# Sparse attention's projections in another order: index block first, one query block of 512 columns, score scratch in another pool

## The chip, the cores and the metric

The kernel runs on one core of a Trainium2 chip. A core has five engines, each with its own instruction queue that it works through strictly in the order in which the program was built: TensorE (PE in the profile; its weight loads are PEld), VectorE (DVE), ScalarE (ACT), GpSimd (POOL) and SyncE (SP, which here only starts transfers). Engines wait for one another by semaphores. The metric is the device time of one execution in microseconds (us).

## The reference

Two layers of a decoder trunk over 512 tokens of width 1024, in float32. Cut to what matters here:

```python
h = rmsnorm(x, norm_mix)
(a_x, a_b, a_c, d_q, d_k, d_v, i_q, i_k, i_w, ..., m_q, gate_logits) = split_cols(h @ w_in)
y_a = a_b * causal_conv3(a_c * a_x, conv_w)             # branch A
# branch B, sparse attention, for each block of 128 queries:
rel   = relu(iq . ik * 64**-0.5)                        # 8 index heads
score = sum over heads of rel * iw                      # (128, keys), causal
sel   = top_k(score, 128)                               # the 128 best keys of each query
out   = softmax(q . k[sel] / 8) @ v[sel]                # 8 heads of 64
# branch C: gated recurrence; branch M: cross-attention into 256 memory tokens
merged = sum over the branches of sigmoid(gate) * (y_branch @ w_lift)
x = x + merged @ w_out
x = x + (silu(gate) * up) @ ffn_w_down                  # feed-forward
```

Columns of `w_in` that belong to sparse attention: 512 for the queries `d_q`; 64 + 64 for `d_k` and `d_v`; 512 + 64 + 8 for the indexer `i_q`, `i_k`, `i_w`.

## The kernel before

Every product of the two operands' full precision is three matmuls of rounded halves (`mm3`, L324, L325, L327: high by high, low by high, high by low). A weight chunk (`Chunk`, made by `wchunk`) is loaded by SP into `w_raw`, ACT rounds it to `w_hi` (L100, the line of the helper `A`), and DVE makes the remainder `w_lo` (L257). There are 4 buffers of `w_raw` and 3 each of `w_hi` and `w_lo`. `features` computes with weights as the stationary operand, 512 tokens moving; `tokens` and `tokens_wide` with a tile of 128 tokens as the stationary operand and the weight's columns moving, so that a matmul is as wide as the chunk has columns.

In a layer's `mixer` several generators are woven together. `script(EARLY[l], ...)` names one step per letter: `b` projections of sparse attention, `c` convolution branch, `m` memory branch, `s` a step of the selection, `n` (layer 1 only) the late norm. After it, `lift(3, ...)` (gates and lift of the memory branch; four rounds of 48 gate matmuls on h and 24 on y) is woven with what is left of the selection, and then `values` and `lift(0, ...)` with `attend(0)` to `attend(3)`.

- `projections` has a key block of 256 columns (`d_k`, `d_v` and the first two index heads), an index block of 456 columns, and the queries as two blocks of 256. Each block's results are scaled out of PSUM by ACT into a tile `wide` (4 buffers) and then normalised, rotated and turned per head (`key_heads`, `index_heads`, `query_heads`; mostly DVE, with transposes on PE).
- `select(t)`, for t = 1 to 3, works on n = 128(t+1) keys. For each of 8 heads: a product of two matmuls on PE (`dots`, L841 and L842, into a PSUM tile `at`, 2 buffers), a relu by ACT into a scratch tile, and one DVE instruction that adds it to `score` (L994, L996). Then 16 rounds on DVE of MAX8 (L1002) and MATCH_REPLACE8 (L1003), and a mask `bias` (L1006).
- `attend(t)` makes logits (`dots` again, on `qS` and `k`), then on DVE the maximum with mask (L857), on ACT the exponential, on DVE a reciprocal (L860), on ACT the scaling of `prob`, and on PE its transposes (L871). The first of them stands on PE behind the first half of the first gates of `lift(0)`.

All of this gives only the priorities. The order in which instructions stand on each engine is set when the program is built, by a scheduler with a timeline of its own (`TileContext(nc, schedule_with_timeline_sim=True)`); instructions under `tc.high_priority` come earlier, and `tc.add_manual_dep(..., order)` pins single pairs. On the chip nothing is reordered.

Of the kernel before, what the change touches and what calls it, by code (L numbers as in the profile page):

```python
# [16 lines left out]
AF = mybir.ActivationFunctionType  # L17
# [6 lines left out]
NT = S // P  # L24
D = 1024
KD = D // P
# [11 lines left out]
C_AX, C_AB, C_AC, C_DQ, C_DK, C_IQ, C_IK = 0, 512, 1024, 1536, 2048, 2176, 2688  # L38
# [3 lines left out]
NONC = -2.0e38  # L42
OFF = -1.0e30
AHEAD = 3000
EARLY = ["mmbmcmcbmmmscsmcsssmccmbs", "mnmbmcmcbmmmscsmcsssmccmbs"]
MM_BUFS = 3
TR_BUFS = 3
AT_BUFS = 2
# [23 lines left out]
def hybrid_trunk(ctx: ExitStack, tc: tile.TileContext, x, mem, positions, norm_mix, w_in, conv_w,  # L72
# [33 lines left out]
    def mm_ps():  # L106
        return pmm.tile([P, 512], F32, name="mm")
# [4 lines left out]
    def tr_ps():  # L112
        return pat.tile([P, 512], F32, name="tr", bufs=TR_BUFS)
# [32 lines left out]
    ps = tr_ps()  # L146
# [16 lines left out]
    ps = tr_ps()  # L163
# [64 lines left out]
    class Chunk:  # L228
        def __init__(self, src, kt, n):
            self.kt, self.step = kt, min(kt, 1024 // n)  # L230
            self.parts = []
            for k in range(0, kt, self.step):
                e = min(kt, k + self.step)
                m = (e - k) * n
                raw, hi, lo = (wpool.tile([P, 1024], dt, name=nm, bufs=b)[:, :m].rearrange("p (k n) -> p k n", n=n)
                               for nm, dt, b in (("w_raw", F32, RAW_BUFS), ("w_hi", F32R, W_BUFS), ("w_lo", F32R, W_BUFS)))
                if len(src.shape) == 2:
                    loaded[0] = nc.sync.dma_start(raw, src[k * P:e * P].rearrange("(k p) n -> p k n", p=P))
                    raw_loads.append(loaded[0])
                    if len(raw_loads) == 2:  # L240
                        tc.add_manual_dep(mem_half.ins, loaded[0].ins.name, order, reason="weights first")
                    if keys:
                        tc.add_manual_dep(loaded[0].ins, keys.pop().ins.name, order, reason="keys first")
                else:
                    for g in range(2):
                        nc.sync.dma_start(raw.rearrange("p k (g c) -> p k g c", g=2)[:, :, g, :], src[:, k:e, g, :])
                with tc.high_priority(offset=AHEAD):
                    if len(raw_loads) == 1:
                        dve.tensor_copy(hi[:, 1:, :], raw[:, 1:, :])
                        i = A(hi[:, :1, :], raw[:, :1, :], AF.Copy)  # L250
                    else:
                        i = A(hi, raw, AF.Copy)
                    while len(self.parts) == 1 and before_second:
                        tc.add_manual_dep(i.ins, before_second.pop().ins.name, order, reason="probabilities first")
                    while behind:
                        tc.add_manual_dep(i.ins, behind.pop().ins.name, order, reason="accumulators first")
                    i2 = dve.tensor_sub(lo, raw, f(hi))  # L257
                    while low_after:
                        tc.add_manual_dep(low_after.pop().ins, i2.ins.name, order, reason="weights first")
                    while low_behind:  # L260
                        tc.add_manual_dep(i2.ins, low_behind.pop().ins.name, order, reason="operands first")
                    while after_hi:
                        tc.add_manual_dep(after_hi.pop().ins, i.ins.name, order, reason="weights first")
                    for a in after_two:
                        tc.add_manual_dep(a.ins, i.ins.name, order, reason="weights first")
                    for a in after_los:
                        tc.add_manual_dep(a.ins, i2.ins.name, order, reason="weights first")
                self.parts.append((range(k, e), hi, lo))
            after_two.clear()
            after_los.clear()  # L270
# [9 lines left out]
    def wchunk(src, kt, n):  # L280
        return Chunk(src, kt, n)
# [17 lines left out]
    def tokens(w, a, t, ps, k0=0, kt=None, first=0):  # L299
        kt = w.kt if kt is None else kt  # L300
        for k in range(k0 + first, k0 + w.kt):
            mm3(ps, pair(a, k, slice(t * P, (t + 1) * P)), w.at(k - k0), k == 0, k == kt - 1)
# [52 lines left out]
    def scratch512(n):  # L355
        return state.tile([P, S], F32, name="sq", bufs=2)[:, :n]
# [93 lines left out]
    h = new_h()  # L450
# [183 lines left out]
    def mixer(l, h, norms, cm):  # L634
# [197 lines left out]
        with pool_("dsa") as dp:  # L832
# [60 lines left out]
            with pool_("idx") as ip:  # L893
# [5 lines left out]
                def wide():  # L899
                    return ip.tile([P, S], F32, name="wide", bufs=4)  # L900
# [63 lines left out]
                def index_out(ps, t):  # L964
                    u = wide()
                    with tc.high_priority(offset=AHEAD):
                        A(u[:, :7 * HD], ps[:, :7 * HD], AF.Copy, scale=r_t[:, t:t + 1])
                        A(iw[:, t, :], ps[:, 7 * HD:7 * HD + 8], AF.Copy, scale=r8_t[:, t:t + 1])
                    return u

                def index_heads(u, t):
                    w = by_head(u)
                    rope(w[:, :7], 7, t)
                    dve.tensor_copy(w[:, 7, :], w[:, 6, :])
                    ps = turn_heads(u, 4)
                    twin_to(ikS, ps[:, 3 * P:], t)
                    heads_to(iqS, 2, ps[:, :3 * P], 6, t)

                def query_heads(u, t):
                    w = by_head(u)  # L980
                    headnorm(w, 8, gq_b[l])
                    rope(w, 8, t)
                    heads_to(qS, 0, turn_heads(u, 4), 8, t)

                def select(t):
                    n = (t + 1) * P
                    score = ip.tile([P, S], F32, name="score", bufs=1)[:, :n]
                    for hh in range(8):
                        ps = at_ps()[:, :n]
                        dots(ps, iqS, ikS, hh, t, n)  # L990
                        rel = wide()[:, :n]
                        A(rel, ps, AF.Relu, scale=HD ** -0.5)
                        if hh == 0:
                            dve.tensor_scalar(score, rel, iw[:, t, 0:1], 0.0, op0=OP.mult, op1=OP.add)  # L994
                        else:
                            dve.scalar_tensor_tensor(score, rel, iw[:, t, hh:hh + 1], score, op0=OP.mult,  # L996
                                                     op1=OP.add)
                    dve.copy_predicated(score[:, t * P:], future, neg.to_broadcast([P, P]))
                    yield
                    for i in range(TOPK // 8):  # L1000
                        m8 = ip.tile([P, 16], F32, name="m8", bufs=2)[:, :8]
                        dve.max(m8, score)  # L1002
                        dve.match_replace(score, m8, score, REPL)  # L1003
                        if i % 4 == 3:
                            yield
                    dve.tensor_scalar(biases[t], score, REPL, OFF, op0=OP.not_equal, op1=OP.mult)  # L1006

                def projections():
                    w = wchunk(w_in[l][:, C_DK:C_DK + 256], KD, 256)
                    for t in range(NT):  # L1010
                        ps = mm_ps()[:, :256]
                        tokens(w, h, t, ps)
                        key_heads(key_out(ps, t), t)
                    yield
                    w = wchunk(w_in[l][:, C_DK + 256:C_DK + 712], KD, 456)
                    pss = [mm_ps()[:, :456] for _ in range(MM_BUFS)] + [tr_ps()[:, :456]]
                    tokens_wide([w], h, KD, pss, in_turn=True)
                    for t, u in enumerate([index_out(ps, t) for t, ps in enumerate(pss)]):
                        index_heads(u, t)
                    yield  # L1020
                    us = [wide() for _ in range(NT)]
                    for c in range(2):
                        w = wchunk(w_in[l][:, C_DQ + c * 256:C_DQ + (c + 1) * 256], KD, 256)
                        for t in range(NT):
                            ps = mm_ps()[:, :256]
                            tokens(w, h, t, ps)
                            with tc.high_priority(offset=AHEAD):
                                A(us[t][:, c * 256:(c + 1) * 256], ps, AF.Copy, scale=r_t[:, t:t + 1])
                            if c:
                                query_heads(us[t], t)  # L1030
                    yield

                y_m, y_a = new_y(), new_y()
# [651 lines left out]
```

## Time and profile before

| | |
|---|---|
| median of 3 runs | 1975.92 us (1974.9 to 1976.09) |
| profiled execution | 1974.79 us, span 1972.8 us |
| granted PE clock | 0.998 of full speed |
| PE busy | 99% of the span, 9687 matmuls |
| DVE busy | 74% |
| ACT busy | 59% |
| POOL busy | 12% |
| transfers | 385.25 MB, mean 195 GB/s |

Matmuls are pipelined and the profile models their ends, so one matmul's duration (0.39 us for 512 columns) is longer than the distance from its start to the next one's start; what a matmul costs in a full queue is that distance. Instructions of DVE and ACT overlap a little at their ends as well, and are read the same way. Layer 0's mixer lies between about 70 and 690 us, layer 1's between about 1024 and 1640 us.

### The profile page before, as it was taken

What the parts mean: (1) busy time and instruction counts of PE and PEld (TensorE: products, weight loads), DVE (VectorE), ACT (ScalarE), POOL (GpSimd) and SP (SyncE); (2) the same over time, 40 slices, a digit from 0 to 9 for tenths busy, and PEclk for the clock granted to TensorE, in tenths of its full rate; (3) what the DMA queues carried; (4) which work ended last, traced back from release to release, by engine and by line L of the source; (5) the groups of instructions that cost most, each with busy time, mean ns of one, the idle gap of its engine ahead of it and who ended that gap; (6) DMA issues with size and microseconds to landing.
All of it is one profiled execution on the core that took longest, in us unless ns stands there. A gap on an engine that the chain in (4) does not pass through costs nothing.

```text
span 1972.8 us, 26656 instructions
## 1 busy us (share of the span) xinstructions
PE 1958.9 (99%) x9687; PEld 1636.0 (83%) x9687; DVE 1466.6 (74%) x2569; ACT 1169.3 (59%) x1958; POOL 236.2 (12%) x288
## 2 busy tenths in 40 slices
PE   9999999999999999999999999999999999999999
PEld 8888987878888888888888898878888888888887
DVE  7866998657876677786876699965678667867777
ACT  6754654766765456645654556477667655656564
POOL 1011111111111111100001111111111110111000
PEclk9999999999999999999999999999999999999999
DMA  8677666667687888886677767677777778898754
GB/s 304 207 179 168 172 160 166 161 139 172 166 210 186 231 232 255 244 245 188 202 218 168 181 144 174 148 182 157 167 177 162 209 198 251 250 266 235 213 186 139
DMA packets 222228, 385.25 MB, mean 195 GB/s; under 512 B 13194, under 2 KB 118224, under 8 KB 221840
## 3 DMA queue, kind: packets, MB, share of 16 engines
q1 hardware_dynamic: 163008, 244.16, 39.3%
q0 software_dynamic: 52192, 132.81, 33.3%
q10 hardware_dynamic: 6896, 6.58, 1.0%
q8 instruction: 76, 1.25, 0.3%
q14 instruction: 56, 0.46, 0.1%
HBM read 368.81 MB, written 140.51 MB: 258 GB/s over the span
## 4 chain that ended last, share of the span: by engine, by line
PE 97%; DVE 3%; ACT 0%; issue 0%; DVEq 0%; ACTq 0%
PE mm L327 24%; PE mm L324 23%; PE mm L325 23%; PE at L324 4%; PE at L325 4%; PE at L327 4%; PE tr L324 2%; PE tr L327 2%; PE tr L325 2%; PE tr L871 1%; PE tr L882 1%; PE tr L1577 1%; DVE score L1003 1%; PE at L842 1%; PE at L841 1%; DVE m L1002 1%
## 5 line engine op out<-in xcount | busy, mean ns | idle before, releaser
L100 ACT ACTIVATE w_hi<-w_raw 128x1024 fp32r<-128x1024 f32 (+1 forms) x435 | 457.3, 1054 | 353.1 <-PE mm L325 113.3
L324 PE MATMUL mm<-h_hi,w_hi 128*128 128x512 f32 x960 | 377.4, 394 | 0.6 <-DVE zg L1076 0.6
L325 PE MATMUL mm<-h_lo,w_hi 128*128 128x512 f32 x960 | 376.6, 392 | 0.0
L327 PE MATMUL mm<-h_hi,w_lo 128*128 128x512 f32 x960 | 374.8, 397 | 0.7 <-DVE w_lo L257 0.7
L1288 DVE TENSOR_TENSOR w_lo<-w_raw,w_hi 128x1024 fp32r<-128x1024 f32 x211 | 256.3, 1218 | 130.0 <-ACT w_hi L100 129.3
L257 DVE TENSOR_TENSOR w_lo<-w_raw,w_hi 128x1024 fp32r<-128x1024 f32 (+1 forms) x224 | 272.2, 1217 | 105.4 <-ACT w_hi L100 103.9
L1303 POOL DMA_DIRECT2D up_sums<-in_ffn_w_up_dram x120 | 121.5, 1012 | 836.5 <-DMA up_sums<-in_ffn_w_up_dram 554.6
L327 PEld LDWEIGHTS mm<-h_hi,w_lo 128*128 128x128 f32 x960 | 182.7, 190 | 37.6 <-DVE w_lo L257 0.8
L324 PEld LDWEIGHTS mm<-h_hi,w_hi 128*128 128x128 f32 x960 | 180.4, 188 | 36.3 <-issue 1.0
L325 PEld LDWEIGHTS mm<-h_lo,w_hi 128*128 128x128 f32 x960 | 180.4, 188 | 35.6 <-issue 0.2
L325 PE MATMUL mm<-w_lo,h_hi 128*128 128x512 f32 (+2 forms) x488 | 169.4, 347 | 0.3 <-DVE w_lo L257 0.3
L327 PE MATMUL mm<-w_hi,h_lo 128*128 128x512 f32 (+2 forms) x488 | 169.5, 347 | 0.0
L324 PE MATMUL mm<-w_hi,h_hi 128*128 128x512 f32 (+2 forms) x488 | 163.8, 347 | 0.0
L1303 POOL DMA_DIRECT2D w_sums<-in_ffn_w_down_dram x66 | 62.3, 944 | 331.8 <-DMA w_sums<-in_ffn_w_down_dram 186.2
L325 PEld LDWEIGHTS mm<-w_lo,h_hi 128*128 128x128 f32 x488 | 92.3, 189 | 11.3 <-DVE w_lo L257 0.6
L324 PEld LDWEIGHTS mm<-w_hi,h_hi 128*128 128x128 f32 x488 | 92.3, 189 | 10.5 <-ACT w_hi L100 0.2
L327 PEld LDWEIGHTS mm<-w_hi,h_lo 128*128 128x128 f32 x488 | 92.3, 189 | 10.2
L100 ACT ACTIVATE prob<-prob,small 128x128 f32<-128x128 f32 (+3 forms) x128 | 68.8, 554 | 33.6 <-DVE small L857 24.5
L327 PE MATMUL mm<-y_hi,w_lo 128*128 128x512 f32 x192 | 75.5, 393 | 0.0
L325 PE MATMUL mm<-y_lo,w_hi 128*128 128x512 f32 x192 | 75.4, 393 | 0.0
L324 PE MATMUL mm<-y_hi,w_hi 128*128 128x512 f32 x192 | 75.4, 393 | 0.0
L325 PE MATMUL mm<-w_lo,a_hi 128*128 128x512 f32 x160 | 63.2, 395 | 0.0
(496 smaller groups left out, 4191.6 us busy)
## 6 DMA issues: line engine op xcount, KB each, us to landing
w_raw<-in_w_in_dram SPq DMA_DIRECT2D x140, 512.0 KB, 4.6
up_sums<-in_ffn_w_up_dram POOLq DMA_DIRECT2D x120, 512.0 KB, 7.0
w_raw<-up_sums SPq DMA_DIRECT2D x80, 512.0 KB, 5.3
w_raw<-in_ffn_w_up_dram SPq DMA_DIRECT2D x60, 512.0 KB, 4.6
w_sums<-in_ffn_w_down_dram POOLq DMA_DIRECT2D x54, 512.0 KB, 6.1
up_sums<-up_sums POOLq DMA_DIRECT2D x40, 512.0 KB, 5.1
w_raw<-in_w_lift_dram SPq DMA_DIRECT2D x32, 512.0 KB, 4.6
w_raw<-in_ffn_w_down_dram SPq DMA_DIRECT2D x24, 512.0 KB, 5.0
```

What stands on the lines that cost most here:

```text
L100: i = act.activation(dst, src, func, **kw)
L257: i2 = dve.tensor_sub(lo, raw, f(hi))
L324: made += [pe.matmul(ps, ah, bh, start=first, stop=False, skip_group_check=more), pe.matmul(ps, ah, bl, start=False, stop=False, skip_grou ...
L325: pe.matmul(ps, ah, bl, start=False, stop=False, skip_group_check=more)]
L327: made += [pe.matmul(ps, al, bh, start=False, stop=last, skip_group_check=more)]
L841: return [pe.matmul(ps, q[:, hh, s], k[0][:, :n], start=True, stop=False), pe.matmul(ps, q[:, hh, s], k[1][:, :n], start=False, stop=True)]
L842: pe.matmul(ps, q[:, hh, s], k[1][:, :n], start=False, stop=True)]
L871: turn = pe.transpose(pp[:, (2 * e + i) * P:(2 * e + i + 1) * P], probs[2 * i + e][:, b * P:(b + 1) * P], ident)
L882: i = pe.matmul(pv[e * HD:(e + 1) * HD, c], vt[:, b, :], pt[:, b, e * 2 * P:(e + 1) * 2 * P], start=b == 0, stop=b == t)
L1002: dve.max(m8, score)
L1288: two = A(hi, raw, AF.Copy), dve.tensor_sub(lo, raw, f(hi))
L1303: i = nc.gpsimd.dma_start(dst, src, **kw)
```

## The change

The index block comes first, then the key block. The queries become one block of 512 columns over four accumulators (three `mm` tiles and one `tr` tile of PSUM), taken out by a new function `query_out`, and each token tile's `query_heads` is a step of its own, so that steps of other branches can lie between. The scratch of the relu in `select` moves from the pool `wide` (4 buffers) to `scratch512`, a tile `sq` with 2 buffers. The two letter strings change, and the pinned orders `after_two` and `after_los` hold only for a chunk's first part.

```diff
-EARLY = ["mmbmcmcbmmmscsmcsssmccmbs", "mnmbmcmcbmmmscsmcsssmccmbs"]
+EARLY = ["mbmmbcmmmsccbsmcmsssmmsbbcbbc", "mnbmmbcmmmsccbsmcmsssmmsbbcbbc"]
...
-                    for a in after_two:
+                    for a in after_two if len(self.parts) < 2 else []:
                         tc.add_manual_dep(a.ins, i.ins.name, order, reason="weights first")
-                    for a in after_los:
+                    for a in after_los if len(self.parts) < 2 else []:
                         tc.add_manual_dep(a.ins, i2.ins.name, order, reason="weights first")
...
+                def query_out(ps, t):
+                    u = wide()
+                    with tc.high_priority(offset=AHEAD):
+                        A(u, ps, AF.Copy, scale=r_t[:, t:t + 1])
+                    return u
...
-                        rel = wide()[:, :n]
+                        rel = scratch512(n)
                         A(rel, ps, AF.Relu, scale=HD ** -0.5)
...
                 def projections():
+                    w = wchunk(w_in[l][:, C_DK + 256:C_DK + 712], KD, 456)
+                    pss = [mm_ps()[:, :456] for _ in range(MM_BUFS)] + [tr_ps()[:, :456]]
+                    tokens_wide([w], h, KD, pss, in_turn=True)
+                    for t, u in enumerate([index_out(ps, t) for t, ps in enumerate(pss)]):
+                        index_heads(u, t)
+                    yield
                     w = wchunk(w_in[l][:, C_DK:C_DK + 256], KD, 256)
...
-                    w = wchunk(w_in[l][:, C_DK + 256:C_DK + 712], KD, 456)
-                    pss = [mm_ps()[:, :456] for _ in range(MM_BUFS)] + [tr_ps()[:, :456]]
+                    w = wchunk(w_in[l][:, C_DQ:C_DQ + 512], KD, 512)
+                    pss = [mm_ps() for _ in range(MM_BUFS)] + [tr_ps()]
                     tokens_wide([w], h, KD, pss, in_turn=True)
-                    for t, u in enumerate([index_out(ps, t) for t, ps in enumerate(pss)]):
-                        index_heads(u, t)
-                    yield
-                    us = [wide() for _ in range(NT)]
-                    for c in range(2):
-                        w = wchunk(w_in[l][:, C_DQ + c * 256:C_DQ + (c + 1) * 256], KD, 256)
-                        for t in range(NT):
-                            ps = mm_ps()[:, :256]
-                            tokens(w, h, t, ps)
-                            with tc.high_priority(offset=AHEAD):
-                                A(us[t][:, c * 256:(c + 1) * 256], ps, AF.Copy, scale=r_t[:, t:t + 1])
-                            if c:
-                                query_heads(us[t], t)
+                    for t, u in enumerate([query_out(ps, t) for t, ps in enumerate(pss)]):
+                        yield
+                        query_heads(u, t)
                     yield
```

How the built order changes is shown at two places of layer 0; layer 1 reads the same way. The first is PE at the last two products of `select(3)`, its seventh and eighth head. Before, they stand within the lift (`y` operands) of the last round of `lift(3)`, ahead of all matmuls of `values`:

```order
L325 MATMUL mm_3394<-y_lo_796,w_hi_3389 128x512
L327 MATMUL mm_3394<-y_hi_795,w_lo_3390 128x512
L324 MATMUL mm_3394<-y_hi_795,w_hi_3389 128x512
L841 MATMUL at_3024<-ik_hi_791,iqS_790 128x512
L842 MATMUL at_3024<-ik_lo_792,iqS_790 128x512
L841 MATMUL at_3030<-ik_hi_791,iqS_790 128x512
L842 MATMUL at_3030<-ik_lo_792,iqS_790 128x512
L325 MATMUL mm_3394<-y_lo_796,w_hi_3389 128x512
L327 MATMUL mm_3394<-y_hi_795,w_lo_3390 128x512
L324 MATMUL mm_3395<-y_hi_795,w_hi_3389 128x512
```

Now they stand on PE behind three quarters of `values` (`w`, `h` operands; `w_hi_3347` belongs to the fourth and last part of its weights):

```order
L841 MATMUL at_2920<-ik_hi_791,iqS_790 128x512
L842 MATMUL at_2920<-ik_lo_792,iqS_790 128x512
L324 MATMUL tr_3355<-w_hi_3341,h_hi_146 128x512
L325 MATMUL tr_3355<-w_lo_3342,h_hi_146 128x512
L327 MATMUL tr_3355<-w_hi_3341,h_lo_147 128x512
L324 MATMUL mm_3352<-w_hi_3347,h_hi_146 128x512
L324 MATMUL mm_3353<-w_hi_3347,h_hi_146 128x512
L841 MATMUL at_2926<-ik_hi_791,iqS_790 128x512
L842 MATMUL at_2926<-ik_lo_792,iqS_790 128x512
L324 MATMUL mm_3354<-w_hi_3347,h_hi_146 128x512
```

Counted in 512-column matmuls, 142 stood between the eighth product and the first `prob` transpose of `attend(0)` (14 of the lift, 96 of `values`, 32 of the first gates); now it is 54 (22 and 32). The fifth and sixth products also stand within `values` now; the first four still stand within `lift(3)`.

The second place is DVE at the last `merged` instruction of `lift(3)` (L682), where `score_...` is `select(3)` unless said otherwise. Before, all eight heads had been added to the score by then, and the first round of the selection follows:

```order
L682 TENSOR_TENSOR merged_2825<-gate_3322,mm_3394 128x512
L996 SCALAR_TENSOR_TENSOR score_2987<-wide_3021,iw_794,score_2987 128x512
L996 SCALAR_TENSOR_TENSOR score_2987<-wide_3027,iw_794,score_2987 128x512
L222 SCALAR_TENSOR_TENSOR gate_e_3382<-gate_3323,gate_e_3382 128x512
L996 SCALAR_TENSOR_TENSOR score_2987<-wide_3033,iw_794,score_2987 128x512
L257 TENSOR_TENSOR w_lo_3446<-w_raw_3444,w_hi_3445 128x1024
L998 COPY_PREDICATED score_2987<-future_96,neg_89 128x128
L682 TENSOR_TENSOR merged_2825<-gate_3323,mm_3395 128x512
L1002 MAX m8_3037<-score_2987 128x8
L1003 MATCH_REPLACE score_2987<-m8_3037,score_2987 128x512
```

Now DVE ends `select(2)` there (`score_2407`), and all eight heads of `select(3)` (`score_2883`) come behind it:

```order
L1009 MATCH_REPLACE score_2407<-m8_2879,score_2407 128x384
L1012 TENSOR_SCALAR bias2_785<-score_2407 128x384
L682 TENSOR_TENSOR merged_2721<-gate_3219,mm_3291 128x512
L1000 TENSOR_SCALAR score_2883<-sq_2887,iw_794 128x512
L1002 SCALAR_TENSOR_TENSOR score_2883<-sq_2893,iw_794,score_2883 128x512
L1002 SCALAR_TENSOR_TENSOR score_2883<-sq_2899,iw_794,score_2883 128x512
L1002 SCALAR_TENSOR_TENSOR score_2883<-sq_2905,iw_794,score_2883 128x512
L1002 SCALAR_TENSOR_TENSOR score_2883<-sq_2911,iw_794,score_2883 128x512
L257 TENSOR_TENSOR w_lo_3348<-w_raw_3346,w_hi_3347 128x1024
L1002 SCALAR_TENSOR_TENSOR score_2883<-sq_2917,iw_794,score_2883 128x512
```

(In the changed kernel's numbering L1000, L1002, L1008, L1009 and L1012 are the lines that were L994, L996, L1002, L1003 and L1006.) In both, the mask of `attend(0)` (L857) follows on DVE only behind `bias3`. The products of `select(1)` moved the other way: ahead of the first of them stood 226 matmuls of the convolution on PE, and now 158.

## The prediction

> **What bounds the kernel now.** I read the page first: busy shares, then the chain that ended last.
>
> ```profile
> span 1972.8 us, 26656 instructions
> PE 1958.9 (99%) x9687; PEld 1636.0 (83%) x9687; DVE 1466.6 (74%) x2569; ACT 1169.3 (59%) x1958; POOL 236.2 (12%) x288
> PE 97%; DVE 3%; ACT 0%; issue 0%; DVEq 0%; ACTq 0%
> ```
>
> PE is the bound: it is idle for 1972.8 - 1958.9 = 13.9 us in all, and the chain runs on it but for 3% on DVE. Two things can therefore move the time: what PE has to do, and the places where it waits. Who makes it wait is in the view of waits of PE (total, times, longest), and where, in the busy times by stretch (PE, PEld, DVE, ACT, POOL, then granted clock):
>
> ```profile
> PE tr L871 <- ACT prob L100: 5.7, 2, 3.5
> 80.00:130.00 50.00, 50.00 (x272) 44.26 (x271) 33.55 (x92) 24.10 (x63) 4.92 (x6) 1.00 0.56 145
> 200.00:260.00 60.00, 60.00 (x376) 54.30 (x376) 55.21 (x132) 37.43 (x77) 9.44 (x11) 1.00 0.67 164
> 300.00:335.00 35.00, 31.54 (x141) 25.93 (x140) 30.87 (x67) 10.76 (x22) 4.24 (x6) 0.97 0.63 144
> 1260.00:1290.00 30.00, 27.04 (x121) 21.95 (x121) 26.88 (x60) 9.82 (x20) 4.46 (x5) 0.98 0.65 139
> ```
>
> The wait is one per layer, at the first transpose of a probability of `attend(0)` (L871). DVE is slack early in a mixer (33.55 of 50 us) and nearly full later (55.21 of 60). The lines around that wait, in order of time on PE, ACT and DVE:
>
> ```profile
> 294.67 0.39 PE L842 MATMUL at<-ik_lo,iqS 128*128 128x512 f32 x1
> 295.12 0.39 PE L842 MATMUL at<-ik_lo,iqS 128*128 128x512 f32 x1
> 332.09 0.33 PE L871 MATMUL tr<-ident,prob 128*128 128x128 f32 x1 [3.46 <-ACT prob L100]
> 332.17 5.50 PE L327 MATMUL mm<-h_hi,w_lo 128*128 128x512 f32 x16
> 337.51 0.39 PE L324 MATMUL mm<-y_hi,w_hi 128*128 128x512 f32 x1
> ...
> 295.09 0.60 ACT L100 ACTIVATE wide<-at 128x512 f32<-128x512 f32 x1
> ...
> 301.58 0.69 DVE L1002 MAX8 m<-score 128x8 f32<-128x512 f32 x1
> 310.58 0.69 DVE L1002 MAX8 m<-score 128x8 f32<-128x512 f32 x1
> 312.10 0.69 DVE L1002 MAX8 m<-score 128x8 f32<-128x512 f32 x1
> 327.27 0.43 DVE L1006 TENSOR_SCALAR bias<-score 128x512 f32<-128x512 f32 x1
> ```
>
> At 294.67 and 295.12 the seventh and eighth products of `select(3)` end (their second matmuls start there). DVE selects from 301.58 to 327.27, and only behind that, in its queue, comes the mask of `attend(0)` on which the transpose hangs at 332.09. PE has run out of work 3.46 us before. `attend(0)` needs nothing of `select(3)`; it stands behind it in DVE's queue. Layer 1 shows the same, with its 2.97 us in two pieces:
>
> ```profile
> 1250.97 0.39 PE L842 MATMUL at<-ik_lo,iqS 128*128 128x512 f32 x1
> 1285.17 0.50 PE L327 MATMUL mm<-h_hi,w_lo 128*128 128x512 f32 x1 [0.69 <-DVE w_lo L257]
> 1287.95 0.33 PE L871 MATMUL tr<-ident,prob 128*128 128x128 f32 x1 [2.28 <-ACT prob L100]
> ```
>
> From the eighth product to that transpose it takes 332.09 - 295.12 = 36.97 us in layer 0 and 36.98 us in layer 1.
>
> **The matmuls.** The query projection has 4 token tiles, 8 parts of the depth and 3 matmuls: 96 of 512 columns a layer instead of 192 of 256. What each costs is the distance of starts:
>
> ```profile
> 200.41 0.28 PE L327 MATMUL mm<-w_hi,h_lo 128*128 128x256 f32 x1
> 200.53 0.28 PE L324 MATMUL mm<-w_hi,h_hi 128*128 128x256 f32 x1
> 296.03 0.39 PE L325 MATMUL mm<-y_lo,w_hi 128*128 128x512 f32 x1
> 296.25 0.39 PE L327 MATMUL mm<-y_hi,w_lo 128*128 128x512 f32 x1
> 298.52 0.39 PE L324 MATMUL mm<-w_hi,h_hi 128*128 128x512 f32 x1
> ```
>
> A 256-column one takes 0.12 us; from 296.03 to 298.52 are 11 of 512 columns, 0.2267 us each. So 96 x (2 x 0.12 - 0.2267) = 1.28 us a layer, 2.55 us in all, is saved on the bound itself. The Trainium skill's page "TensorE: Matmul & The Clock Gate", section "Back-to-back issue gap", gives N / 2.4 + 2.5 ns for a lone stream, by which a pair of 256 costs only 2.5 ns more than one of 512: an estimate of 0.5 us saved in all, and a sum 2.1 us higher than mine. The trace's own distances are about 11 ns longer at both widths, and I take those.
>
> **The eighth product, placed later on PE.** Between it and the transpose stood 142 matmuls of 512 columns, now 54. The 88 others now run before it, so it starts 88 x 0.2267 = 19.95 us later, less the 1.28 us.
>
> **The chain behind it.** Before, DVE was not waiting for that product: it was busy with the lift. Now it comes to the eighth head with nothing else to do, because the fifth to eighth heads' products all stand within `values`. Durations for the steps:
>
> ```profile
> L996 DVE SCALAR_TENSOR_TENSOR score<-wide,iw,score 128x512 f32<-128x512 f32 x14 | 10.5, 748 | 0.3
> L100 ACT ACTIVATE wide<-at 128x512 f32<-128x512 f32 x16 | 9.0, 591 | 0.2
> 300.73 0.35 DVE L998 COPY_PREDICATED_SCALAR score<-future,neg 128x128 f32 x1
> ```
>
> From the product's second matmul to its relu 295.09 - 294.67 = 0.42; the relu 0.59; the addition to the score 0.75; the causal copy 0.35; 16 rounds at 312.10 - 310.58 = 1.52 each, 24.3; from the mask of `select(3)` to the transpose 332.09 - 327.27 = 4.82, as now. Together 31.2 us. PE's own work in that time is 54 x 0.2267 = 12.2 and about 1.1 for the eight small logit matmuls and the last product, so it stands idle for some 17.9 us at L871, where it stood 3.46 and 2.97. No cover is left: what follows on PE needs the low halves of the weights (L257), which stand behind the same queue of DVE.
>
> **A bank freed later.** The third accumulator of `values` is the bank of the last lift product, free when DVE's last `merged` (L682) is done.
>
> ```profile
> 300.99 0.68 DVE L682 TENSOR_TENSOR merged<-gate,mm 128x512 f32<-128x512 f32 x1
> L1002 DVE MAX8 m<-score 128x8 f32<-128x384 f32 x32 | 17.9, 558 | 0.6
> L1003 DVE MATCH_REPLACE8 score<-m,score 128x384 f32<-128x384 f32 x32 | 17.4, 543 | 0.0
> ```
>
> PE needs it 18 matmuls behind 298.52, at 302.60; the next DVE instruction starts at 301.58, so there is 1.0 us to spare. Between the last gate (L665) and that L682, DVE now has four MAX8 (0.5 as distance of starts) and five replacements (0.65 with their loads) of 384 keys and a mask (0.4), for five score additions and a copy before (3.8): 1.8 us more. Three matmuls fewer lie ahead of PE's need: 0.7 us. So 1.8 + 0.7 - 1.0, about 1.4 us of new wait a layer; between 0 and 3.
>
> **The smaller parts.** Behind ACT's fifth relu, which waits for its product, stands the rounding of the last part of `values` (`w_hi`), and behind DVE's fifth addition its `w_lo`. Both are reckoned done some 3 us before PE needs them: 0, at most 2 a layer. The heads' transposes of the index block come some 0.6 us sooner behind their matmuls than before: 0 to 1. The scratch with 2 buffers ties relu, addition and product closer; where DVE keeps up, as it does in rounds 1 to 3 of the lift, it costs 0. ACT takes four blocks of 512 out in place of eight of 256, off the path (ACT is at 59%). The weight loads are ten a layer as before, in another order in SP's queue; PE waits for no transfer in the list of waits, and POOL's queue keeps its order: 0. The loosened pins touch the first chunk of layer 0 alone: 0, within 0.5 either way. When PE comes back from a stall it is slow: 16 matmuls take 337.51 - 332.17 = 5.34 us instead of 3.63. That is paid once per stall now and stays so, unless the longer stall shifts it by up to 1.7 us a layer.
>
> **The sum.** Layer 0: the eighth product at 295.12 + 19.95 - 1.28 + 1.4 = 315.2, the transpose 31.2 later at 346.4, against 332.09: 14.3 us later. Layer 1: 1250.97 + 20.07 + 31.2 = 1302.2 against 1287.95: 14.3 again. Behind the transposes both orders read alike and PE is full, so nothing is given back. 28.6 us on the profiled execution's 1974.79 make 2003.4; the median of the runs is 1.1 us above that execution, so 2004. With the bounds above (each layer 12 to 18) it is 1998 to 2011.
>
> **Rivals.**
> *Products done early after all.* If the heads five to eight were not limited by where PE issues them, DVE would go straight on behind L682 at about 301.4 (301.58 + 1.8 - 0.7 - 1.28): eight additions 5.8, a `w_lo` 1.2, copy and rounds 24.6, 4.8 to the transpose, 337.8, or 5.7 later a layer: 1987. It decides by whether those products can leave PE before DVE is ready; the built order puts them 11 to 18 us behind the lift's end, and an engine does not reorder. 5%.
> *The ring of two locks PE, ACT and DVE together.* Then each of the last four products costs PE 0.42 + 0.59 + 0.75, up to 7 us a layer on top: up to 2018. For it: ACT's relu of a third product must wait for DVE's addition of the first, and weights wait behind it on ACT. Against: between those products stand up to 20 matmuls, 4.5 us. 6%.
> *Faster.* The products of `select(1)` stand 68 convolution matmuls, 15 us, earlier, in the stretch where DVE is a third idle. If that empties DVE's backlog so that `select(3)` ends before PE reaches L871, both stalls go, with their slow restarts: 1974.8 - 2.55 - 3.46 - 2.97 - 3.4 = 1962.4, and 1963.5 by the median. The point is whether DVE can finish within the 13.3 us that PE has left behind the eighth product, and 31.2 do not fit. 4%.
> *Nothing measurable*: the saved matmuls and a little less backlog against a little more wait, within 0.2% (4 us, about what a measurement of this kernel can tell from no change). It needs a stall of 2 to 6 us where I have 17.9. 2%.
>
> **Chances.** 83% for the forecast (1998 to 2011). Faster 4%, same 2%, slower 94% (forecast and first two rivals). The range 1996 to 2014 leaves out the two fast rivals, the first one and the upper half of the second.
>
> **What the changed profile would show.** Right: at the first L871 of each layer a wait of 16 to 20 us for ACT's `prob`, PE idle in all near 45 us; the eighth 512-key product near 315 us; on DVE idle time before the additions of the last heads (waits on ACT's `sq`), then 16 unbroken rounds of 1.52 us to about 341; 256-column matmuls on h down from 576 to 192. A new small wait of `values` for L682 near 300 us. Wrong: if the eighth addition on DVE stands before 305 us, or if the transpose's wait is under 10 us, the placement does not bind and the first rival or the third holds; if PE waits in front of products of `select(2)` or `select(3)`, the ring is the cause.

## The result, and the profile after

The changed kernel takes 2002.2 us (median of 4 runs, 2001.2 to 2003.6) against 1976.0 us of the kernel before: a ratio of 1.0134, 95% interval 1.0117 to 1.0152, so 26.2 us slower. The profiled execution took 2001.21 us, with a span of 1999.1 us. Forecast were 2004 us and 28.6 us more than before.

The page after: span, busy times, and the chain by engine.

```profile
span 1999.1 us, 26273 instructions
PE 1957.7 (98%) x9495; PEld 1626.8 (81%) x9495; DVE 1470.4 (74%) x2569; ACT 1170.1 (59%) x1950; POOL 235.6 (12%) x288
PE 96%; DVE 3%; DMA 0%; ACT 0%; issue 0%; DVEq 0%; ACTq 0%
```

PE is busy 1.2 us less than before, and idle for 41.4 us instead of 13.9. The whole loss is idle time of PE. The view of waits of PE (total, times, longest) says where, and the busy times by stretch (PE, PEld, DVE, ACT, POOL, then granted clock) how it looks around it:

```profile
PE at L841 <- DVE small L857: 28.2, 2, 14.1
PE tr L871 <- ACT prob L100: 6.0, 2, 3.0
```

```profile
80.00:130.00 50.00, 50.00 (x301) 45.13 (x300) 34.52 (x112) 30.35 (x84) 1.55 (x3) 1.00 0.40 117
200.00:260.00 60.00, 60.00 (x295) 50.67 (x294) 48.83 (x94) 36.09 (x72) 9.26 (x10) 1.00 0.72 169
300.00:335.00 35.00, 26.74 (x120) 21.86 (x119) 26.08 (x51) 9.80 (x14) 4.88 (x6) 0.95 0.51 117
```

Each layer has one stall in two pieces: 14.1 us at the second pair of logits of `attend(0)` (L841), which needs an `at` buffer that the row maximum (L857) frees, and 3.0 us at the first transpose (L871): 17.1 us where before had 3.5 and 3.0. Between 300 and 335 us DVE is not full either (26.08 of 35 us): it waits first, and then runs the rounds. On PE, in layer 0 from the last lift matmul to the restart, and the same steps in layer 1:

```profile
295.29 0.39 PE L327 MATMUL mm<-y_hi,w_lo 128*128 128x512 f32 x1
...
313.65 0.39 PE L842 MATMUL at<-ik_lo,iqS 128*128 128x512 f32 x1
...
340.86 0.47 PE L841 MATMUL at<-k_hi,qS 128*128 128x128 f32 x1 [14.12 <-DVE small L857]
...
344.99 0.48 PE L871 MATMUL tr<-ident,prob 128*128 128x128 f32 x1 [3.02 <-ACT prob L100]
345.12 5.65 PE L327 MATMUL mm<-h_hi,w_lo 128*128 128x512 f32 x16
...
1282.25 0.39 PE L842 MATMUL at<-ik_lo,iqS 128*128 128x512 f32 x1
...
1309.45 0.48 PE L841 MATMUL at<-k_hi,qS 128*128 128x128 f32 x1 [14.12 <-DVE small L857]
...
1313.58 0.48 PE L871 MATMUL tr<-ident,prob 128*128 128x128 f32 x1 [3.01 <-ACT prob L100]
```

From the eighth product (L842) to the first L871 it is 31.34 and 31.33 us. DVE in layer 0 at the same time:

```profile
299.99 0.68 DVE L682 TENSOR_TENSOR merged<-gate,mm 128x512 f32<-128x512 f32 x1
300.59 0.48 DVE L1000 TENSOR_SCALAR score<-sq,iw 128x512 f32<-128x512 f32 x1
301.10 2.47 DVE L1002 SCALAR_TENSOR_TENSOR score<-sq,iw,score 128x512 f32<-128x512 f32 x3
307.68 0.75 DVE L1002 SCALAR_TENSOR_TENSOR score<-sq,iw,score 128x512 f32<-128x512 f32 x1 [4.10 <-ACT sq L100]
...
313.12 0.75 DVE L1002 SCALAR_TENSOR_TENSOR score<-sq,iw,score 128x512 f32<-128x512 f32 x1 [2.60 <-ACT sq L100]
314.71 0.75 DVE L1002 SCALAR_TENSOR_TENSOR score<-sq,iw,score 128x512 f32<-128x512 f32 x1 [0.84 <-ACT sq L100]
315.49 0.36 DVE L1004 COPY_PREDICATED_SCALAR score<-future,neg 128x128 f32 x1
315.89 0.69 DVE L1008 MAX8 m<-score 128x8 f32<-128x512 f32 x1
...
340.17 0.43 DVE L1012 TENSOR_SCALAR bias<-score 128x512 f32<-128x512 f32 x1
340.51 0.28 DVE L857 CUSTOM_DVE_ANT_0 prob<-at,causal_bias 128x128 f32<-128x128 f32 x1
```

The first four heads are added right behind the lift; for the fifth, seventh and eighth DVE waits 4.10, 2.60 and 0.84 us, and then come the 16 rounds, 24.3 us from 315.89 to 340.17. Only then does `attend(0)` get its row maximum.

### The profile page after: what moved, and what is told of

It reads as the page before. It is cut to its first block, busy times and chain, and to the rows that moved or that the text cites. A ratio compares the mean times of both kernels' runs of the same rounds, so it can differ in the third digit from the quotient of the medians.

```text
span 1999.1 us, 26273 instructions
## 1 busy us (share of the span) xinstructions
PE 1957.7 (98%) x9495; PEld 1626.8 (81%) x9495; DVE 1470.4 (74%) x2569; ACT 1170.1 (59%) x1950; POOL 235.6 (12%) x288
## 4 chain that ended last, share of the span: by engine, by line
PE 96%; DVE 3%; DMA 0%; ACT 0%; issue 0%; DVEq 0%; ACTq 0%
PE mm L327 24%; PE mm L324 23%; PE mm L325 23%; PE at L324 4%; PE at L327 4%; PE at L325 4%; PE tr L324 2%; PE tr L327 2%; PE tr L325 2%; DVE score L1009 1%; DVE m L1008 1%; PE tr L871 1%; PE tr L882 1%; PE tr L1579 1%; PE at L842 1%; PE at L841 1%
## 5 line engine op out<-in xcount | busy, mean ns | idle before, releaser
L100 ACT ACTIVATE w_hi<-w_raw 128x1024 fp32r<-128x1024 f32 (+2 forms) x435 | 457.5, 1054 | 349.5 <-PE mm L325 102.4
L327 PE MATMUL mm<-w_hi,h_lo 128*128 128x512 f32 (+2 forms) x408 | 152.1, 373 | 0.0
L325 PE MATMUL mm<-w_lo,h_hi 128*128 128x512 f32 (+2 forms) x408 | 151.6, 372 | 0.1
L324 PE MATMUL mm<-w_hi,h_hi 128*128 128x512 f32 (+2 forms) x408 | 146.4, 373 | 0.0
L325 PEld LDWEIGHTS mm<-w_lo,h_hi 128*128 128x128 f32 x408 | 76.9, 188 | 12.8 <-DVE w_lo L257 0.5
L324 PEld LDWEIGHTS mm<-w_hi,h_hi 128*128 128x128 f32 x408 | 76.9, 188 | 12.2 <-ACT w_hi L100 0.2
L327 PEld LDWEIGHTS mm<-w_hi,h_lo 128*128 128x128 f32 x408 | 76.8, 188 | 12.0
```

The source lines that it names most:

```text
L100: i = act.activation(dst, src, func, **kw)
L324: made += [pe.matmul(ps, ah, bh, start=first, stop=False, skip_group_check=more), pe.matmul(ps, ah, bl, start=False, stop=False, skip_grou ...
L325: pe.matmul(ps, ah, bl, start=False, stop=False, skip_group_check=more)]
L327: made += [pe.matmul(ps, al, bh, start=False, stop=last, skip_group_check=more)]
```

## The experiments

The theory to begin with: the eighth product is late on PE, 31 us of DVE and ACT work hang on it, and `attend(0)` stands behind that work in DVE's queue. Rivals: the two-buffer scratch ties three engines together; the new strings, or the query block, cost the time in another way; the DVE work is needed, and its place doesn't matter. Times are medians, beside 1974.5 to 1974.9 us of the kernel before in the same rounds.

**Half the rounds.**

```diff
-                    for i in range(TOPK // 8):
+                    for i in range(TOPK // (16 if t == NT - 1 else 8)):
```

> The changed kernel, but select(3) runs 8 of its 16 rounds of maximum and replacement (the mask of the last 128 queries then keeps fewer keys). Theory (the 31.3 us chain on DVE from the eighth product to attend(0) sets PE's stall): 8 x 1.52 = 12.2 us of 17.1 us of stall go in each layer, so 2002.2 - 24.3 = 1978 us, and some 5 us of stall a layer are left at L841 and L871. Rival (the scratch with two buffers, which ties PE, ACT and DVE together, sets the end): the rounds are off the path and the time stays within 4 us of 2002.

1977.75 us (ratio to before 1.0013, 1.0004 to 1.0023). The waits of PE:

```profile
PE tr L871 <- ACT prob L100: 9.4, 2, 6.3
PE at L841 <- DVE small L857: 2.0, 1, 2.0
```

5.7 us a layer are left where 4.9 were expected. The rounds are on the path that sets the end, one for one.

**The scratch back in `wide`.**

```diff
-                        rel = scratch512(n)
+                        rel = wide()[:, :n]
```

> The changed kernel with the relu's scratch put back into the four buffers of wide. In the built order the eighth product of select(3) then has 80 matmuls of 512 columns between it and the first L871, where the changed kernel has 54. Theory (the place of the eighth product on PE decides): it starts 26 x 0.2267 = 5.9 us earlier, the stall is 11.2 us a layer instead of 17.1, and the time 2002.2 - 11.8 = 1990 us. Rival A (the scratch is the whole cause): both stalls fall to the 3 us of before, 1974 us. Rival B (the blocks' order and the query block are the whole cause): 2002 us.

1992.2 us (ratio 1.0087, 1.0070 to 1.0104): the theory's value within 2.2 us, and far from both rivals. PE of this kernel in layer 0:

```profile
308.08 0.39 PE L842 MATMUL at<-ik_lo,iqS 128*128 128x512 f32 x1
...
336.70 0.47 PE L841 MATMUL at<-k_hi,qS 128*128 128x128 f32 x1 [9.63 <-DVE small L857]
...
340.82 0.47 PE L871 MATMUL tr<-ident,prob 128*128 128x128 f32 x1 [3.02 <-ACT prob L100]
```

The product comes 5.6 us earlier (5.9 expected), and the chain is 32.7 us instead of 31.3, since a `w_lo` now stands between the last two additions:

```profile
309.40 1.23 DVE L257 TENSOR_TENSOR w_lo<-w_raw,w_hi 128x1024 fp32r<-128x1024 f32 x1 [0.19 <-ACT w_hi L100]
310.55 0.75 DVE L1002 SCALAR_TENSOR_TENSOR score<-wide,iw,score 128x512 f32<-128x512 f32 x1
```

**The old strings.**

```diff
-EARLY = ["mbmmbcmmmsccbsmcmsssmmsbbcbbc", "mnbmmbcmmmsccbsmcmsssmmsbbcbbc"]
+EARLY = ["mmbmcmcbmmmscsmcsssmccmbs", "mnmbmcmcbmmmscsmcsssmccmbs"]
```

> The changed kernel with the two strings of before that set the order of the steps; blocks, accumulators and scratch stay as changed. In the built order 114 matmuls of 512 columns stand between the eighth product and the first L871. Theory: by the product alone the stall is 31.3 - (114 x 0.2267 + 2.0) = 3.5 us a layer; by DVE (two additions, a copy, 16 rounds and a w_lo behind the last L682) some 4 to 5; so 2002.2 - 2 x (12 to 13.6), 1975 to 1978 us, and up to 3 us less if the shorter stall also shortens PE's slow restart. Rival (the two-buffer scratch is the cause): at least 1990 us.

2006.8 us (ratio 1.0161, 1.0146 to 1.0176): the theory is wrong by 30 us. The time would fit the rival (at least 1990 us), but the waits of PE do not, since none stands at the scratch:

```profile
PE tr L808 <- DVE mprob L806: 16.9, 6, 3.4
PE tr L871 <- ACT prob L100: 6.7, 2, 3.5
PE at L841 <- DVE small L857: 3.6, 2, 1.8
PE at L324 <- DMA mv<-kv: 3.2, 1, 3.2
```

The stall of `attend(0)` did shrink as reckoned, to 5.1 us a layer. In its place stands another at L808, where the memory branch turns its probabilities, which neither theory had, and one wait of 3.2 us for a transfer of the same branch. PE is also busy 8 us more (1965.8 against 1957.7). Between 200 and 222 us, where stalls follow one another closely, the granted clock is 0.77; behind a single stall of 2.1 us that ends at 78.8 us it is 1.00 (78 to 84 us).

**`attend(0)` first on DVE.** `last_rounds` holds the maxima of `select(3)`, `first_peaks` the second L857 of `attend(0)`, and `order` means an order without a semaphore.

```diff
-                    score = ip.tile([P, S], F32, name="score", bufs=1)[:, :n]
+                    score = dp.tile([P, S], F32, name="score", bufs=1)[:, :n]
...
-                        m8 = ip.tile([P, 16], F32, name="m8", bufs=2)[:, :8]
+                        m8 = dp.tile([P, 16], F32, name="m8", bufs=2)[:, :8]
...
+                for i in last_rounds:
+                    tc.add_manual_dep(i.ins, first_peaks[0].ins.name, order, reason="attention first")
```

> The changed kernel, with one order added on DVE: every maximum of select(3) stands behind the second row maximum of attend(0). For that, score and m8 lie in the outer pool, since attend's pool opens only where the index pool closes. The eighth product stays late on PE (55 matmuls of 512 columns ahead of the first L871). Theory (attend(0) waits for select(3) only because it stands behind it on DVE): both stalls go, 2 x 17.1 us and up to 3.4 us of slow restarts, so 1964.5 to 1968 us; the rounds fill DVE's idle third during attend(0) and attend(1). Rival (the DVE work is needed and the wait only moves): a new wait of PE at attend(1) to attend(3) for L857 or bias3, of 5 to 17 us a layer, 1975 to 2002 us.

1970.5 us (ratio to before 0.9976, 0.9967 to 0.9986), 31.7 us less than the changed kernel, with the eighth product as late as there, and 2.5 us above the theory's range. Both stalls are gone. A little of the rival is there as well: a new wait for `prob` in each layer, 4.0 us in the two together, in layer 0 at 428 us in `attend(3)`. Its cause was not pursued.

```profile
PE tr L873 <- ACT prob L100: 4.0, 2, 2.1
```

L873 is here the line that was L871.

**The same on the kernel before.** The same edit.

> The kernel before, with the same added order on DVE as in the run that put attend(0) first (score and m8 in the outer pool, every maximum of select(3) behind the second row maximum of attend(0)). Theory (the 6.4 us of stall at L871 and L327 are DVE's queue as well): they go, with up to 3.4 us of slow restarts, less the 2 us a layer that the changed kernel kept at the first transpose: 1968 to 1974 us by the 1976 of before. If the late products were all that the changed kernel lost by, this one and that run (1970.5) agree but for the matmuls saved: 1971 to 1973. Rival (what the changed kernel won in that run came from its other parts, the earlier select(1) and fewer matmuls): no gain here, 1975 to 1978.

1971.0 us (ratio 0.9979, 0.9971 to 0.9988), within the expectation. The stalls of before were of the same kind.

**The scratch alone.** In the kernel before:

```diff
-                        rel = wide()[:, :n]
+                        rel = scratch512(n)
```

> The kernel before, with the relu of the scores in the two-buffer scratch, nothing else. In the built order the eighth product has 123 and 124 matmuls of 512 columns behind it ahead of the first L871, where before has 142 and 143. Theory: 31.3 - (124 x 0.2267 + 2.0) = 1.2 us of stall from the product, so DVE's own backlog (3.5 us, as now) still ends last: 1976 us, within 4. Rival (the scratch of two locks PE, ACT and DVE together): 2 to 7 us a layer more, 1980 to 1990.

1977.6 us (ratio 1.0014, 1.0005 to 1.0023), nearer to the theory. The wait at L871 grows to 8.1 us in all from 5.7:

```profile
PE tr L871 <- ACT prob L100: 8.1, 2, 4.6
```

**The query block alone.** In the kernel before:

```diff
-                    us = [wide() for _ in range(NT)]
-                    for c in range(2):
...
+                    w = wchunk(w_in[l][:, C_DQ:C_DQ + 512], KD, 512)
+                    pss = [mm_ps() for _ in range(MM_BUFS)] + [tr_ps()]
+                    tokens_wide([w], h, KD, pss, in_turn=True)
+                    for t, u in enumerate([query_out(ps, t) for t, ps in enumerate(pss)]):
+                        query_heads(u, t)
```

> The kernel before, with the query projection as one block of 512 over four accumulators, nothing else (heads without the yields between them). The eighth product has 123 matmuls of 512 columns behind it. Theory: no product is late (1.4 us by the product, 3.5 by DVE), and 96 x (2 x 0.12 - 0.2267) = 1.28 us a layer are saved: 1973.5 us, within 3. With a matmul's cost by columns alone (2.5 ns a matmul saved) it is 1975.5. Rival (the four accumulators taken at once cost the change its time): 1980 us or more.

1998.8 us (ratio 1.0122, 1.0108 to 1.0135): wrong by 25 us, in the direction of the rival, but not at the accumulators. The waits of PE, and the stretch of layer 0 that holds them:

```profile
PE tr L808 <- DVE mprob L806: 11.0, 5, 2.8
PE tr L871 <- ACT prob L100: 6.8, 2, 3.5
PE at L841 <- DVE small L857: 3.7, 2, 1.8
```

```profile
200.00:222.00 22.00, 15.91 (x70) 13.13 (x68) 17.75 (x56) 5.91 (x14) 3.69 (x4) 0.77 0.63 145
```

The place is again L808. Ahead of each head's transposes there the memory branch has a chain from PE over DVE, ACT and DVE back to PE, which other matmuls must cover. Counted in the built order of layer 0 (neighbouring rows that read alike as one), between one group of these transposes and the next stand 116, 66, 136, 84, 180, 88 and 93 other rows on PE before; here 116, 66, 136, 84, 172, 18, 12 and 17. The two waits of layer 0, 2.75 and 2.59 us, stand behind the 18 and the 12 rows. The query matmuls that lay between the last steps, two blocks of 256, now all stand ahead of them. The run with the old strings has the same 18, 12 and 17, and 17 at the start as well. The changed kernel, whose strings are new, has 64 or more everywhere, and no wait at L808. So the strings repair what the query block breaks; that the count of covering rows is the cause was read from the two orders and the waits, not tried by itself.

**Both: query block and `attend(0)` first, in the kernel before.**

> The kernel before with both the query block of 512 and attend(0) ahead of select(3)'s rounds on DVE. Theory: the gains of the two runs add up: 2.5 us below the one with the order alone, 1966 to 1972 us, the fastest of all here. Rival: with PE never waiting, the remaining time is PE's matmuls, and this run, the changed kernel with attend(0) first (1970.5) and the one before with it agree within 3 us.

1986.7 us (ratio 1.0058, 1.0043 to 1.0074): the expectation falls with the one before it. Only the memory branch's stall is left, and it is of the same size:

```profile
PE tr L808 <- DVE mprob L806: 11.7, 5, 3.3
```

**The scores' place alone.** The run with `attend(0)` first had two edits. Here is the changed kernel with the two tiles moved and no order added:

```diff
-                    score = ip.tile([P, S], F32, name="score", bufs=1)[:, :n]
+                    score = dp.tile([P, S], F32, name="score", bufs=1)[:, :n]
...
-                        m8 = ip.tile([P, 16], F32, name="m8", bufs=2)[:, :8]
+                        m8 = dp.tile([P, 16], F32, name="m8", bufs=2)[:, :8]
```

> The changed kernel with score and m8 in the outer pool, without the added order on DVE: the other half of the edit that put attend(0) first. In the built order 55 matmuls of 512 columns stand behind the eighth product, where the changed kernel has 54. Theory (the order on DVE's queue made the gain of 31 us): the stalls stay at 17 us a layer, 2002 us. Rival (it was the memory's place that tied attend(0) to select(3)): the stalls go, 1965 to 1975.

1964.5 us (ratio 0.9947, 0.9934 to 0.9961): the theory falls, and the rival holds, 0.5 us below its range. No kernel run here is faster; the last two below agree with it. The page, and DVE in layer 0:

```profile
span 1962.0 us, 26267 instructions
PE 1953.8 (100%) x9495; PEld 1624.7 (83%) x9495; DVE 1461.4 (74%) x2569; ACT 1171.0 (60%) x1950; POOL 235.9 (12%) x288
```

```profile
316.13 0.69 DVE L1008 MAX8 m<-score 128x8 f32<-128x512 f32 x1
...
318.71 0.69 DVE L1008 MAX8 m<-score 128x8 f32<-128x512 f32 x1
...
320.44 0.29 DVE L857 CUSTOM_DVE_ANT_0 prob<-at,causal_bias 128x128 f32<-128x128 f32 x1
...
321.32 0.28 DVE L857 CUSTOM_DVE_ANT_0 prob<-at,causal_bias 128x128 f32<-128x128 f32 x1
...
362.75 0.43 DVE L1012 TENSOR_SCALAR bias<-score 128x512 f32<-128x512 f32 x1
```

On PE the eighth product is as late as in the changed kernel:

```profile
313.89 0.39 PE L842 MATMUL at<-ik_lo,iqS 128*128 128x512 f32 x1
...
327.99 0.27 PE L871 MATMUL tr<-ident,prob 128*128 128x128 f32 x1
```

From it to the first L871 it is now 14.1 us, PE's own work, instead of 31.3. The row maxima of `attend(0)` stand between the rounds, without being told to. The rounds stretch to 362.75 us, which is early enough for what needs `bias3`. In the code, `score` and `m8` belong to the index pool (`ip`), and the pools of `values` and `attend` open where that pool has closed. So as long as these two tiles are in it, the order that is built has no use of the later pools on DVE ahead of the last round. In the built kernel the addresses of `score` and `m8` overlap none of those of `hv` (the results of `values`), `prob` and `pt` (the turned `prob`), which speaks for the pool as a whole and against reuse of these two tiles' own memory. That was not tried apart.

**`attend(0)` first, with the scratch in `wide`.** Both edits above on the changed kernel, and the relu back in `wide`.

> The changed kernel with the relu's scratch back in wide and attend(0) ahead of select(3)'s rounds on DVE. 48 matmuls of 512 columns stand behind the eighth product. Theory: with the mask of attend(0) off select(3)'s chain, the place of the products and the scratch's buffers matter no more: 1970.5 us, within 2.5. Rival (the two-buffer scratch still costs something beside the stalls): 1963 to 1967, the fastest of all.

1965.5 us (ratio 0.9953, 0.9939 to 0.9966): 5 us below the theory, and within the rival's range. The rival's reason does not hold by itself, though: without the added order the scratch makes no difference (1964.9 against 1964.5 us, in the last run below). It is the added order that costs time, and not equally: 6.0 us in the changed kernel (1970.5 against 1964.5), 6.2 us in the kernel before (1971.0 against 1964.8), and 0.7 us here (1965.5 against 1964.9). Late products do not explain it, since in the kernel before they come earliest. The order lets DVE stand idle until `attend(0)` has its logits: in the kernel before with the order, DVE has its last score ready at 301.3 us and makes the first round at 321.3 us, with 15.4 us of idle time between. The new wait of PE for `prob` goes the same way as the cost: 4.0 us in the changed kernel, 2.4 us in the kernel before, 0.4 us here. Why it is so small here stays open.

**The scores' place alone, in the kernel before**, and **in the changed kernel with the scratch in `wide`**: the same two moved tiles.

> The kernel before, with score and m8 in the outer pool and nothing else; the same move took the changed kernel from 2002.2 to 1964.5 us. The eighth product has 142 matmuls of 512 columns behind it, as before. Theory (attend's pool opens only behind select(3), which reads score in the pool that closes there; that alone makes attend(0) wait): the 6.4 us of stall and some 3 us of slow restarts go, 1965 to 1967.5 us. The difference to 1964.5 is then what the rest of the change brings: by the rows 2.55 us of matmuls, so 1967.1; by the columns alone 0.5, so 1965.0. Rival (before's stalls come from DVE's backlog and not from the pool): 1972 to 1975.

> The changed kernel with score and m8 in the outer pool and the relu's scratch back in wide. Theory: PE waits for nothing of select(3), so neither the place of its products nor the scratch's buffers show: 1964.5 us, within 1.5. Rival (the scratch's two buffers cost something by themselves): 1960 to 1962.5.

1964.8 us (ratio 0.9951, 0.9939 to 0.9963) and 1964.9 us (0.9951, 0.9937 to 0.9964). With the pool out of the way, before and changed kernel agree within 0.3 us, which no run here tells apart, and the scratch doesn't matter. Of the two values that were expected for the kernel before, 1967.1 us by the distances of starts and 1965.0 us by the columns, the time is nearer to the second. The page of the kernel before with the tiles moved:

```profile
span 1963.3 us, 26656 instructions
PE 1956.2 (100%) x9687; PEld 1634.7 (83%) x9687; DVE 1463.0 (75%) x2569; ACT 1169.8 (60%) x1958; POOL 235.5 (12%) x288
```

PE's busy time there is 2.4 us above that of the changed kernel with the same edit, and the span 1.3 us: the latter waits 0.9 and 0.6 us for `pt` at L871 and L882, where the former lists no such wait.

## Why the prediction was right, and where it was not

- *The matmuls* (2.55 us saved in all): PE's busy times with the stalls gone differ by 2.4 us, near the 2.55 us by the trace's distances of starts. The 0.5 us estimated by the formula for an isolated matmul in the Trainium skill's page "TensorE: Matmul & The Clock Gate", section "Back-to-back issue gap", is far from it. The ends of matmuls are modelled, though: the spans differ by 1.3 us, since new waits take up the rest, and the medians by 0.3 us, less than the 0.9 us by which runs of one of these kernels differ. So the saving is seen on PE, and not shown in the time.
- *The eighth product, later on PE* (315.2 us): 313.65. Without the bank's 1.4 us the sum gives 313.8; the count of 88 matmuls was right to 0.2 us.
- *The chain behind it* (31.2 us): 31.34 and 31.33. Halving the rounds and moving the product show that the rounds count one for one and that the stall follows the product; the smaller terms were not tried by themselves.
- *A bank freed later* (1.4 us a layer): 0. PE waits for nothing near 300 us. This term was mis-sized because it took the distance of 18 matmuls from the order of before. In the changed order 44 matmuls stand between the last lift matmul at 295.29 and the first use of that accumulator, so PE gets there at 295.29 + 45 x 0.2267 = 305.5, and the bank is free at 299.99 + 0.68. The bounds, 0 to 3, held it.
- *The stall* (17.9 us at L871): 17.1 us, but 14.1 of it at the logits ahead of L871. The step overlooked that `at` has two buffers, so that the second pair of logits already needs what L857 frees. It cost nothing by itself: PE has no work between them. It does mean that one of the prediction's own signs of being wrong, a wait of under 10 us at the transpose, came true with 3.0 us, although the mechanism held: with half the rounds, and with the scores' tiles moved, both pieces of the wait shrink or go together.
- *The sum* (14.3 us a layer): the first L871 is 12.90 us later in layer 0, and 25.63 us in layer 1, so 12.73 there. The bank's 1.4 us are nearly all of the difference. The bounds of 12 to 18 us a layer, added up like the forecast, give 1999.9 to 2011.9 us; the range is written as 1998 to 2011, a little lower. The time of 2002.2 us lies within both.
- *The smaller parts*: no wait in the list answers to one of them; the slow restart (16 matmuls in 5.49 us from start to start in layer 0, against 3.63) was there before, with 5.34 us, and stayed.
- *The rivals*: the products did not leave PE early, no wait of PE stands at a product of `select(2)` or `select(3)`, the earlier products of `select(1)` did not let `select(3)` end before PE ran out of work, and nothing was given back.
- *What the argument did not see.* It said that `attend(0)` needs nothing of `select(3)` and stands behind it in DVE's queue. That is so, but it did not ask why. Two tiles in a pool that closes there are the reason; without it the 88 matmuls cost nothing, and both kernels take 1964.5 to 1964.8 us. And it charged the query block with its matmuls alone. By itself that block costs 24 us: 15.6 us of it stay when `attend(0)` comes first (1986.7 against 1971.0), where only the memory branch's stall is left, and the other part goes with the stall at `attend(0)`, which is 10.5 us there against 6.4 before. In the change as a whole there is no wait at L808; the new strings keep 64 rows or more between the branch's steps, which is the likely reason. That this cost and its repair cancel is luck: the prediction had neither.

## What to carry to other kernels

When independent work stands behind a long chain in an engine's queue, look for what put it there before paying for the chain: a tile's pool can order two pieces of work that share no data, and moving the tile outward may be worth more than any order of the steps. A wider block saves its matmuls, but it can also take them away from where they covered another branch's chain; count the rows between that chain's steps in the built order. Take every distance to a buffer's next use from the new order, not from the old one.

## What the runs showed that was not expected

A stall of PE costs more than its length. Taking the changed kernel's stalls away (34.2 us) made it 37.7 us faster. The first 16 matmuls behind each layer's stall took 5.49 us in layer 0 (345.12 to 350.61 us) and 5.85 us in layer 1 (1313.71 to 1319.56 us), from start to start, instead of 3.63: 4.1 us in all. In layer 0 the granted clock is 0.50 from 345.0 to 348.4 us, and 1.00 again from 350 to 355 us. The Trainium skill's page "TensorE: Matmul & The Clock Gate", section "Part 1: The HAM clock gate (the "warmup" mystery)", has the first 3.4 us or so of a busy stretch run at half the clock, by which a restart costs an estimated 1.7 us: near the 1.9 and 2.2 us that the trace shows. In the run with the query block alone the stretch of short stalls shows a granted clock of 0.77, and PE's busy time is 6 us above that of before (1965.0 against 1958.9) with 192 matmuls fewer.
